# Attention matmuls cut from 256 to 128 columns, and the merge's loads given other tiles and another place

## The chip, the cores and the metric

The kernel runs on one core of a Trainium2 chip. The time is device microseconds of one execution of the whole program; several executions are made and the median is quoted. Beside them one execution is profiled, and all views of the profile are of that execution. TensorE is the matrix engine (PE in the profile, its weight loads PEld), VectorE is DVE, ScalarE is ACT, GpSimd is POOL, and SyncE (SP) issues most of the DMAs.

## The reference

One decoder layer on a sequence of 1024 rows of width 1024, in float32. Cut to what matters here:

```python
xn = rmsnorm(x, norm_mix_w)
da_q, da_k, da_v, sw_q, sw_k, sw_v, g_da, g_sw = split_cols(xn @ w_in)
y_da = diff_attention(da_q, da_k, da_v, lam, lam_init, subln_w)   # 4 heads, causal, two softmaxes each
y_sw = sliding_window_attention(sw_q, sw_k, sw_v, sinks)          # 8 heads, window 128
merged = sigmoid(g_da) * (y_da @ w_br_da) + sigmoid(g_sw) * (y_sw @ w_br_sw)
x = x + merged @ w_mix_out
x = x + conv_ffn(rmsnorm(x, norm_ffn_w), w_up, conv_w, conv_b, w_down)
out = rmsnorm(x, norm_final_w)
```

In the first attention a query block of 128 rows sees all keys up to its own block; in the second, its own block and the one before, and the first block only itself.

## The kernel before

Everything is held transposed, channels on the 128 partitions and the 1024 rows along the free axis. A float32 matrix product is made of rounded operands (type fp32r): each operand is split into a high part, which is the value rounded to fp32r by a ScalarE copy, and a low part, which is the value less the high part, a VectorE subtraction. A product is then three matmuls: high by high, high by low, low by high.

The stages follow each other: the projections; the two attentions, with some of the gates' projections (`back_half`, tiles `g`, lines L212 to L214) strewn between as filler for TensorE; the merge (`rest`); the mixing product; the hidden layer; the way down; the last norm. Within a stage a scheduler sets the order of each engine's instructions. It goes by the order in the code, by priorities (`high_priority`), and by when it reckons operands to be ready, so that an edit in one place can reorder rows far around it. Each engine, and each DMA queue, then runs its instructions strictly in that order.

The attention runs six units. Units 0 to 3 are the heads of the first attention. For each of the eight query blocks `da_step` makes scores for both softmaxes (tile `sc`, L639), masks and scales them on VectorE (L643), exponentiates on ScalarE (L644), joins the two (L649), transposes the result on TensorE (L655) and splits it into the tile `aT` (L657, L658). After each second block `da_av` multiplies the pair of blocks, 256 queries wide, by the values (L667 to L669). Of the pair, the earlier block sees one key block less. So in the last key block the first 128 of the 256 columns of `aT` hold nothing; `da_at` has GpSimd write zeros there (L622), and all 256 are multiplied. For the first query block, scores of 256 columns are made though 128 are read (`cuts`). Units 4 and 5 are the second attention: `sw_step` makes 256 columns of scores for each of four heads (L727), also in the first block, where 128 are read.

The merge reads the attention's results back from DRAM (`yd`) into raw tiles `yr` and splits them into `yh` (ScalarE, L836) and `yl` (VectorE, L837): chunks 0 to 3 are the first attention's, 4 to 7 the second's. There are four `yr` tiles, so chunk 4's load waits until chunk 0 is split. For each of eight output blocks m, `first(m)` loads the two gates (tiles `gr`, L796), multiplies them by the row norm on GpSimd (L797), takes the sigmoid (L804), makes the first branch's product (tile `sc`, for m = 0 with the products of the low parts last, L199 to L203) and multiplies it by its gate (L808). `second(m)` makes the second branch's product in two halves (tile `g`, two banks) and multiplies each by its gate (L816), adds the branches (L821) and splits the sum into `mh` and `ml` (L822, L823). `first(0)` and `first(1)` are written ahead of `second(0)`. Gate, result and weight loads all stand in SP's queue; `load_w` (L167, L177, L179) loads and splits a weight block.

Of the kernel before, what the change touches and what calls it, by code (L numbers as in the profile page):

```python
# [10 lines left out]
F32 = mybir.dt.float32  # L11
# [6 lines left out]
P = 128  # L18
D = 1024
T = 1024  # L20
KC = D // P
NB = T // P
H2 = 512
# [21 lines left out]
class Trunk:  # L45
# [568 lines left out]
    def da_at(self, r):  # L614

        t = {}
        for g in range((2 * r + 2 + 3) // 4):
            for part in range(2):
                t[g, part] = self.tl(self.ap, [P, 4, 256], "aT", F32R, bufs=5)
        for part in range(2):  # L620
            j = 2 * r + 1
            self.nc.gpsimd.memset(t[j // 4, part][:, j % 4, 0:P].bitcast(F32), 0.0)  # L622
        return t

    def da_step(self, h, i, st, aT):
        nc, ap = self.nc, self.ap
        q, k = st
        slope = 4.0 ** -(h + 1)
        w = (i + 1) * P

        lo = P if w == 640 else 0
        cuts = ((0, 256),) if i == 0 else ((0, w),) if w <= H2 else ((0, H2 - lo), (H2 - lo, w))
        pr = []
        for c in range(2):
            sc = self.tl(self.psS, [P, T], "sc")
            qs = q[c][:, i * P:(i + 1) * P]
            for part in range(2):
                for n0, n1 in cuts:
                    nc.tensor.matmul(sc[:, lo + n0:lo + n1], qs, k[c][part][:, n0:n1], start=part == 0, stop=part == 1)  # L639
            L = self.tl(ap, [P, T], "L", bufs=4)  # L640
            s = self.tl(self.st, [P, 4], "sm", bufs=8)
            o = 896 - i * P
            nc.vector.tensor_tensor_reduce(L[:, :w], sc[:, lo:lo + w], self.bias[:, o:o + w], slope, 3e38, ALU.add, ALU.min, s[:, 0:1])  # L643
            nc.scalar.activation(L[:, :w], L[:, :w], AF.Exp, bias=s[:, 0:1], scale=-1.0, accum_out=s[:, 1:2] if c else self.s0[:, i:i + 1])  # L644
            pr.append(L)

        nc.vector.reciprocal(s[:, 2:3], s[:, 1:2])
        nc.vector.tensor_scalar(s[:, 3:4], self.s0[:, i:i + 1], s[:, 2:3], self.neglam, ALU.mult, ALU.mult)
        nc.vector.scalar_tensor_tensor(pr[0][:, :w], pr[1][:, :w], s[:, 3:4], pr[0][:, :w], ALU.mult, ALU.add)  # L649
        qo = (i % 2) * P  # L650
        for j0 in range(0, i + 1, 4):
            nj = min(4, i + 1 - j0)
            ps = self.tl(self.psT, [P, 4, P], "t")
            for j in range(nj):
                nc.tensor.transpose(ps[:, j, :], pr[0][:, (j0 + j) * P:(j0 + j + 1) * P], self.ident)  # L655
            hi, lo = aT[j0 // 4, 0], aT[j0 // 4, 1]
            nc.scalar.copy(hi[:, :nj, qo:qo + P], ps[:, :nj, :])  # L657
            nc.vector.tensor_tensor(lo[:, :nj, qo:qo + P], ps[:, :nj, :], hi[:, :nj, qo:qo + P].bitcast(F32), ALU.subtract)  # L658

    def da_av(self, h, r, aT, y):  # L660
        nc = self.nc
        vh, vl = self.vhl
        ps = self.tl(self.psT, [P, H2], "t")
        nj = 2 * r + 2
        for j in range(nj):
            hi, lo = aT[j // 4, 0][:, j % 4, :], aT[j // 4, 1][:, j % 4, :]
            nc.tensor.matmul(ps[:, :256], vh[:, j, :], hi, start=j == 0, stop=False)  # L667
            nc.tensor.matmul(ps[:, :256], vh[:, j, :], lo, start=False, stop=False)  # L668
            nc.tensor.matmul(ps[:, :256], vl[:, j, :], hi, start=False, stop=j == nj - 1)  # L669
        nc.scalar.copy(y[:, r * 256:(r + 1) * 256], ps[:, :256])  # L670

    def da_norm(self, h, y):
# [43 lines left out]
    def sw_step(self, g, n, st):  # L716
        nc, ap = self.nc, self.ap
        q, k = st
        k0 = max(n - 1, 0) * P
        w = P if n == 0 else 256  # L720
        bo = T + (P if n == 0 else 0)
        sc = self.tl(self.psS, [P, 4, 256], "sc")
        s = self.tl(self.st, [P, 4, 4], "sw", bufs=4)
        L = self.tl(ap, [P, 4, 256], "L", bufs=4)
        for h in range(4):
            for part in range(2):
                nc.tensor.matmul(sc[:, h, :], q[h][:, n * P:(n + 1) * P], k[part][:, k0:k0 + 256], start=part == 0, stop=part == 1)  # L727
        for h in range(4):
            slope = 2.0 ** -(4 * g + h + 1)
            nc.vector.tensor_tensor_reduce(L[:, h, :w], sc[:, h, :w], self.bias[:, bo:bo + w], slope, 3e38, ALU.add, ALU.min, s[:, 0, h:h + 1])  # L730
        sink = self.vecs[:, C_SINK + 4 * g:C_SINK + 4 * g + 4]
        nc.vector.tensor_tensor(s[:, 0, :], s[:, 0, :], self.nsink[:, 4 * g:4 * g + 4], ALU.min)
        nc.vector.tensor_tensor(s[:, 1, :], s[:, 0, :], sink, ALU.add)
        nc.scalar.activation(s[:, 1, :], s[:, 1, :], AF.Exp)
        for h in range(4):
            nc.scalar.activation(L[:, h, :w], L[:, h, :w], AF.Exp, bias=s[:, 0, h:h + 1], scale=-1.0, accum_out=s[:, 2, h:h + 1])
        nc.vector.tensor_tensor(s[:, 2, :], s[:, 2, :], s[:, 1, :], ALU.add)
        self.last = nc.vector.reciprocal(s[:, 3, :], s[:, 2, :])
        for h in range(4):
            eng = nc.gpsimd if h in (3,) else nc.vector  # L740
            eng.tensor_scalar(L[:, h, :w], L[:, h, :w], s[:, 3, h:h + 1], None, ALU.mult)
        po = self.tl(self.psT, [P, H2], "t")
        nblk = w // P
        parts = []
        for b in range(nblk):
            ps = self.tl(self.psT, [P, 4, P], "t")
            for h in range(4):
                nc.tensor.transpose(ps[:, h, :], L[:, h, b * P:(b + 1) * P], self.ident)
            pt = self.tl(ap, [P, 2, 4, P], "aT", F32R, bufs=5)
            hi, lo = pt[:, 0], pt[:, 1]  # L750
            nc.scalar.copy(hi, ps)
            nc.vector.tensor_tensor(lo, ps, hi.bitcast(F32), ALU.subtract)
            parts.append((hi, lo))
        for b, (hi, lo) in enumerate(parts):
            kb = k0 // P + b
            va = self.vsw[kb // 4][:, kb % 4, g]
            for m, pt in enumerate((hi, lo)):
                nc.tensor.matmul(po, va, pt, start=b == 0 and m == 0, stop=b == nblk - 1 and m == 1)
        t = self.tl(self.gpool, [P, 4, P], "g", bufs=2)[0:64]
        nc.scalar.copy(t, po[64:128].rearrange("p (h q) -> p h q", h=4))  # L760
        pv = po[0:64].rearrange("p (c e q) -> p c e q", c=2, e=2)
        tv = t.rearrange("p (c e) q -> p c e q", e=2)
        y = self.tl(ap, [P, 2, P], "ys", bufs=3)
        for e in range(2):
            nc.vector.tensor_tensor(y[64 * e:64 * e + 64], pv[:, :, e], tv[:, :, e], ALU.add)
        self.store(self.yd[4 + 2 * g:6 + 2 * g, :, n * P:(n + 1) * P].rearrange("c p q -> p c q"), y)


    def rest(self, gctx):
        nc, tc = self.nc, self.tc  # L770
        with ExitStack() as ctx:
# [3 lines left out]
            with gctx, ExitStack() as bctx:  # L775
                yrp = bctx.enter_context(tc.tile_pool(name="yrp", bufs=4, reuse_waits="tile"))
                yp = bctx.enter_context(tc.tile_pool(name="yp", bufs=1, reuse_waits="tile"))
                bp = bctx.enter_context(tc.tile_pool(name="bp", bufs=2, reuse_waits="tile"))
                parts = []
                for c in range(8):  # L780
                    with tc.high_priority(200):
                        r = self.tl(yrp, [P, T], "yr")
                        nc.sync.dma_start(r, self.yd[c])
                    parts.append(self.split(*(yp.tile([P, T], F32R, name=f"y{p}{c}") for p in "hl"), r))
                    if self.back[7][0]:
                        self.back_half(*self.back[7][0].pop(0))
# [4 lines left out]
                def first(m):  # L791
                    w = self.next_w()
                    gs = []
                    for br in range(2):
                        g = self.tl(bp, [P, T], "gr", bufs=4)
                        nc.sync.dma_start(g, self.gd[8 * br + m])  # L796
                        i = nc.gpsimd.tensor_tensor(g, g, self.rstd, ALU.mult)  # L797
                        if m == 0:

                            tc.add_manual_dep(i.ins, self.last.ins.name, mybir.DependencyInfo(mybir.DependencyClass.Sync, mybir.DependencyReason.DATA),  # L800
                                              reason="softmax first")

                        with tc.issue_after(self.hi.ins) if br else nullcontext():
                            nc.scalar.activation(g, g, AF.Sigmoid)  # L804
                        gs.append(g)
# [654 lines left out]
```

## Time and profile before

| | us |
|---|---|
| median of three runs | 1337.81 (1337.39 to 1337.92) |
| the profiled execution's own time | 1339.47 |
| its span, from the first to the last instruction | 1337.7 |
| busy: TensorE, weight loads | 1319.4, 1096.8 |
| busy: VectorE, ScalarE, GpSimd | 1075.5, 624.4, 483.1 |
| granted TensorE clock, share of full | 0.997 |

The first attention's scores run from about 256 to 390 us, the second's from 390 to 481, and the merge's branch products from 506 to about 597. A row of the timeline gives the start, the time taken, engine, line, operation, the tile written and the tiles read, partitions by elements, the count where equal neighbours are merged, and in brackets how long the engine idled before and what released it. Matmuls overlap in the pipeline: one of 512 columns lasts 0.39 us, while the next one starts 0.23 us after it.

### The profile page before, as it was taken

How to read it: one execution, taken by the hardware profiler on the slowest of the kernel's cores; microseconds unless marked ns; L12 is line 12 of the kernel's file. 1: busy time of each engine (PE TensorE's matmuls, PEld its weight loads, DVE VectorE, ACT ScalarE, POOL GpSimd, SP SyncE). 2: the span in 40 equal slices, each digit the busy share in tenths (PEclk: the TensorE clock that was granted, in tenths of full speed). 3: DMA queues.
4: the chain of work that ended last, by engine and by line, in shares of the span. 5: the costliest groups of instructions: out<-in, count | busy, mean ns of one | idle time of the engine just before them, and what ended most of it. 6: DMA issues, size and time to landing. Idle time of an engine off the chain costs nothing.

```text
span 1337.7 us, 17292 instructions
## 1 busy us (share of the span) xinstructions
PE 1319.4 (99%) x6264; PEld 1096.8 (82%) x6264; DVE 1075.5 (80%) x1607; ACT 624.4 (47%) x1023; POOL 483.1 (36%) x363
## 2 busy tenths in 40 slices
PE   7999999999999999999999999999999999999997
PEld 6888888888888777888888888888888888888887
DVE  8847775289889877765678999999999997879975
ACT  8432232176667766433445443344444444323553
POOL 0336543000102113521436556555565520214532
PEclk9999999999999999999999999999999999999998
DMA  7423443866553335434432222222222229672263
GB/s 259 145 107 142 158 158 142 251 179 174 157 128 125 104 112 212 149 117 132 136 111 84 90 93 82 80 78 95 79 96 75 75 84 332 214 279 67 95 173 126
DMA packets 63621, 183.69 MB, mean 137 GB/s; under 512 B 6960, under 2 KB 15280, under 8 KB 63536
## 3 DMA queue, kind: packets, MB, share of 16 engines
q1 hardware_dynamic: 51504, 164.13, 37.5%
q10 hardware_dynamic: 11456, 17.41, 3.6%
q0 software_dynamic: 576, 1.05, 0.5%
q8 instruction: 49, 0.80, 0.3%
q14 instruction: 36, 0.29, 0.1%
HBM read 130.66 MB, written 50.86 MB: 136 GB/s over the span
## 4 chain that ended last, share of the span: by engine, by line
PE 93%; DVE 3%; POOL 1%; issue 1%; DMA 1%; ACT 1%; POOLq 0%; SPq 0%; ACTq 0%; DVEq 0%
PE t L924 13%; PE t L923 13%; PE t L925 13%; PE g L212 4%; PE g L213 4%; PE g L214 4%; PE sc L213 3%; PE sc L214 3%; PE sc L212 3%; PE t L917 3%; PE sc L639 3%; PE y L1167 2%; PE d L1167 2%; PE d L924 2%; PE d L923 2%; PE d L925 2%
## 5 line engine op out<-in xcount | busy, mean ns | idle before, releaser
L1097 ACT ACTIVATE c<-us,vecs 128x512 f32<-128x512 f32 x80 | 61.3, 781 | 134.0 <-POOL us L1091 130.0
L1099 DVE SCALAR_TENSOR_TENSOR c<-us,vecs,c 128x512 f32<-128x512 f32 x160 | 110.5, 748 | 8.6 <-ACT c L1097 8.6
L1091 POOL TENSOR_TENSOR us<-us,rstd 128x1024 f32<-128x1024 f32 x38 | 99.7, 2643 | 4.5 <-DVE us L472 2.4
L129 DVE TENSOR_TENSOR sl<-sf,sh 128x1024 fp32r<-128x1024 f32 x62 | 86.6, 1399 | 11.5 <-ACT sh L128 11.5
L128 ACT CAST sh<-sf 128x1024 fp32r<-128x1024 f32 x62 | 63.4, 1049 | 59.8 <-PE t L924 43.5
L129 DVE TENSOR_TENSOR wl<-raw,wh 128x1024 fp32r<-128x1024 f32 (+1 forms) x35 | 76.6, 2190 | 3.7 <-ACT wh L128 3.6
L177 ACT CAST wh<-raw 128x1024 fp32r<-128x1024 f32 (+2 forms) x46 | 46.2, 1005 | 67.8 <-PE sc L213 30.4
L104 POOL TENSOR_TENSOR sf<-rv 128x512 f32<-128x512 f32 x30 | 41.3, 1377 | 100.7 <-DVE sl L129 57.8
L212 PE MATMUL g<-xh,wh 128*128 128x512 f32 x176 | 70.7, 402 | 0.1
L214 PE MATMUL g<-xh,wl 128*128 128x512 f32 x176 | 70.4, 400 | 0.0
L213 PE MATMUL g<-xl,wh 128*128 128x512 f32 x176 | 70.2, 399 | 0.0
L179 DVE TENSOR_TENSOR wl<-raw,wh 128x1024 fp32r<-128x1024 f32 (+2 forms) x46 | 53.8, 1169 | 17.5 <-PE t L609 11.0
L109 POOL TENSOR_TENSOR sf<-raw,rv 128x512 f32<-128x512 f32 x30 | 40.8, 1359 | 66.0 <-DVE sl L129 66.0
L643 DVE CUSTOM_DVE_ANT_0 L<-sc,bias 128x128 f32<-128x128 f32 (+7 forms) x64 | 47.8, 752 | 17.0 <-PE sc L639 13.9
L622 POOL MEMSET aT<- 128x128 f32 x32 | 6.2, 205 | 151.6 <-PE t L668 97.9
L797 POOL TENSOR_TENSOR gr<-gr,rstd 128x1024 f32<-128x1024 f32 x16 | 41.0, 2566 | 52.9 <-DMA gr<-gd 43.5
L644 ACT ACTIVATE L<-L,sm 128x128 f32<-128x128 f32 (+7 forms) x64 | 49.6, 779 | 20.0 <-DVE sm L643 13.5
L129 DVE TENSOR_TENSOR wl<-rv,wh 128x512 fp32r<-128x512 f32 x30 | 49.8, 1661 | 3.5 <-ACT wh L128 3.5
L1101 ACT ACTIVATE c<-c 128x512 f32<-128x512 f32 x40 | 24.0, 600 | 60.7 <-DVE c L1099 60.7
L639 PE MATMUL sc<-u,u 128*128 128x512 f32 (+2 forms) x192 | 49.7, 358 | 0.0
L878 POOL TENSOR_TENSOR rstd<-rstd,t 128x512 f32<-128x512 f32 x14 | 21.7, 1558 | 76.1 <-ACT t L877 76.1
L212 PE MATMUL sc<-mh,wh 128*128 128x512 f32 x126 | 49.0, 389 | 0.0
(529 smaller groups left out, 4423.6 us busy)
## 6 DMA issues: line engine op xcount, KB each, us to landing
u<-qd SPq DMA_DIRECT2D x72, 256.0 KB, 6.2
raw<-in_w_in SPq DMA_DIRECT2D x25, 512.0 KB, 4.1
raw<-in_w_up SPq DMA_DIRECT2D x23, 512.0 KB, 3.5
hr<-hd SPq DMA_DIRECT2D x46, 256.0 KB, 5.7
hd<-c SPq DMA_DIRECT2D x22, 512.0 KB, 2.6
rv<-in_w_up SPq DMA_DIRECT2D x21, 512.0 KB, 3.5
raw<-in_w_down SPq DMA_DIRECT2D x19, 512.0 KB, 4.1
gr<-gd SPq DMA_DIRECT2D x16, 512.0 KB, 4.0
```

The source lines that it names most:

```text
L128: i = nc.scalar.copy(hi, src)
L129: j = nc.vector.tensor_tensor(lo, src, hi.bitcast(F32), ALU.subtract)
L212: nc.tensor.matmul(ps, wh[:, kc + o, :], ah, start=first and n == 0, stop=False)
L213: nc.tensor.matmul(ps, wh[:, kc + o, :], al, start=False, stop=False)
L214: nc.tensor.matmul(ps, wl[:, kc + o, :], ah, start=False, stop=last and n == len(kcs) - 1)
L639: nc.tensor.matmul(sc[:, lo + n0:lo + n1], qs, k[c][part][:, n0:n1], start=part == 0, stop=part == 1)
L923: nc.tensor.matmul(ps, ah[:, k, :], bh, start=first and n == 0, stop=False, skip_group_check=skip)
L924: nc.tensor.matmul(ps, ah[:, k, :], bl, start=False, stop=False, skip_group_check=skip)
L925: i = nc.tensor.matmul(ps, al[:, k, :], bh, start=False, stop=last and n == len(ks) - 1, skip_group_check=skip)
L1091: (nc.vector if j == 0 else nc.gpsimd).tensor_tensor(u[:, 2:], u[:, 2:], self.rstd, ALU.mult)
L1097: nc.scalar.activation(c, u[:, o + 2:o + 2 + H2], AF.Identity, bias=self.vecs[:, C_CB + m:C_CB + m + 1], scale=col(m, 2))
L1099: nc.vector.scalar_tensor_tensor(c, u[:, o + k:o + k + H2], col(m, k), c, ALU.mult, ALU.add)
```

## The change

Three things are edited.

First, the last key block's value products in `da_av` read and write only the 128 columns that are used, the zeros in `da_at` go, and the scores of the first query block are made 128 wide in both attentions.

Second, the raw tiles of chunks 4 to 7 come from a pool of their own (`ysp`, four tiles), so that they don't wait for the splits of chunks 0 to 3.

Third, the gates of m = 0 and m = 1 are loaded together, at a higher priority, ahead of chunk 4's load; `first` uses these tiles.

```diff
@@ da_at
-        for part in range(2):
-            j = 2 * r + 1
-            self.nc.gpsimd.memset(t[j // 4, part][:, j % 4, 0:P].bitcast(F32), 0.0)
@@ da_step
-        cuts = ((0, 256),) if i == 0 else ((0, w),) if w <= H2 else ((0, H2 - lo), (H2 - lo, w))
+        cuts = ((0, w),) if w <= H2 else ((0, H2 - lo), (H2 - lo, w))
@@ da_av
-            hi, lo = aT[j // 4, 0][:, j % 4, :], aT[j // 4, 1][:, j % 4, :]
-            nc.tensor.matmul(ps[:, :256], vh[:, j, :], hi, start=j == 0, stop=False)
-            nc.tensor.matmul(ps[:, :256], vh[:, j, :], lo, start=False, stop=False)
-            nc.tensor.matmul(ps[:, :256], vl[:, j, :], hi, start=False, stop=j == nj - 1)
+            c = slice(P if j == nj - 1 else 0, 256)
+            hi, lo = aT[j // 4, 0][:, j % 4, c], aT[j // 4, 1][:, j % 4, c]
+            nc.tensor.matmul(ps[:, c], vh[:, j, :], hi, start=j == 0, stop=False)
+            nc.tensor.matmul(ps[:, c], vh[:, j, :], lo, start=False, stop=False)
+            nc.tensor.matmul(ps[:, c], vl[:, j, :], hi, start=False, stop=j == nj - 1)
@@ sw_step
-                nc.tensor.matmul(sc[:, h, :], q[h][:, n * P:(n + 1) * P], k[part][:, k0:k0 + 256], start=part == 0, stop=part == 1)
+                nc.tensor.matmul(sc[:, h, :w], q[h][:, n * P:(n + 1) * P], k[part][:, k0:k0 + w], start=part == 0, stop=part == 1)
@@ rest
+                ysp = bctx.enter_context(tc.tile_pool(name="ysp", bufs=4, reuse_waits="tile"))
                 parts = []
+                gates = {}
                 for c in range(8):
+                    if c == 4:
+                        with tc.high_priority(300):
+                            for m in range(2):
+                                gates[m] = [self.tl(bp, [P, T], "gr", bufs=4) for _ in range(2)]
+                                for br, g in enumerate(gates[m]):
+                                    nc.sync.dma_start(g, self.gd[8 * br + m])
                     with tc.high_priority(200):
-                        r = self.tl(yrp, [P, T], "yr")
+                        r = self.tl(ysp if c > 3 else yrp, [P, T], "yr")
                         nc.sync.dma_start(r, self.yd[c])
@@ rest, first
-                        g = self.tl(bp, [P, T], "gr", bufs=4)
-                        nc.sync.dma_start(g, self.gd[8 * br + m])
+                        if m in gates:
+                            g = gates[m][br]
+                        else:
+                            g = self.tl(bp, [P, T], "gr", bufs=4)
+                            nc.sync.dma_start(g, self.gd[8 * br + m])
```

The order of the engines' instructions changes as follows. On TensorE, at the first pair of blocks of head 0, this stood before (`t` is the product, `aT` the transposed weights of the softmax, `v` the values, high and low):

```order
L668 MATMUL t_2014<-aT_1968,v_1949 128x256
L669 MATMUL t_2014<-aT_1967,v_1950 128x256
L667 MATMUL t_2014<-aT_1967,v_1949 128x256
L668 MATMUL t_2014<-aT_1968,v_1949 128x256
L669 MATMUL t_2014<-aT_1967,v_1950 128x256
```

The same place now, with line numbers two lower:

```order
L666 MATMUL t_2012<-aT_1968,v_1949 128x256
L667 MATMUL t_2012<-aT_1967,v_1950 128x256
L665 MATMUL t_2012<-aT_1967,v_1949 128x128
L666 MATMUL t_2012<-aT_1968,v_1949 128x128
L667 MATMUL t_2012<-aT_1967,v_1950 128x128
```

The number of matmuls is the same; the last key block's three are half as wide. Counted over the program, 48 value products and 32 scores are 128 wide now, and all 80 were 256 wide before. The order of the rows around them differs on TensorE, VectorE and ScalarE all through the attention.

On SP's queue, at the merge, gates and results stood like this before (the first two `gr` are the gates of m = 0, the next two those of m = 1; the `yr` are chunks 4 to 7):

```order
L796 DMA gr_5078<-gd 128x1024
L796 DMA gr_5082<-gd 128x1024
L783 DMA yr_5044<-yd 128x1024
L783 DMA yr_5050<-yd 128x1024
L783 DMA yr_5056<-yd 128x1024
L783 DMA yr_5062<-yd 128x1024
L796 DMA gr_5118<-gd 128x1024
L796 DMA gr_5122<-gd 128x1024
```

And now:

```order
L786 DMA gr_5015<-gd 128x1024
L786 DMA gr_5016<-gd 128x1024
L786 DMA gr_5019<-gd 128x1024
L786 DMA gr_5020<-gd 128x1024
L789 DMA yr_5023<-yd 128x1024
L789 DMA yr_5029<-yd 128x1024
L789 DMA yr_5035<-yd 128x1024
L789 DMA yr_5041<-yd 128x1024
```

The second pair of gates moved ahead of the four result loads. On VectorE, from chunk 3's split on, before:

```order
L837 TENSOR_TENSOR yl_5041<-yr_5038,yh_5040 128x1024
L179 TENSOR_TENSOR wl_5076<-raw_5072,wh_5074 128x1024
L837 TENSOR_TENSOR yl_5047<-yr_5044,yh_5046 128x1024
L837 TENSOR_TENSOR yl_5053<-yr_5050,yh_5052 128x1024
L837 TENSOR_TENSOR yl_5059<-yr_5056,yh_5058 128x1024
L837 TENSOR_TENSOR yl_5065<-yr_5062,yh_5064 128x1024
L808 TENSOR_TENSOR gr_5078<-gr_5078,sc_5086 128x1024
L808 TENSOR_TENSOR gr_5118<-gr_5118,sc_5126 128x1024
L816 TENSOR_TENSOR gr_5082<-gr_5082,g_5152 128x512
```

And now:

```order
L846 TENSOR_TENSOR yl_5012<-yr_5009,yh_5011 128x1024
L179 TENSOR_TENSOR wl_5055<-raw_5051,wh_5053 128x1024
L817 TENSOR_TENSOR gr_5015<-gr_5015,sc_5061 128x1024
L846 TENSOR_TENSOR yl_5026<-yr_5023,yh_5025 128x1024
L846 TENSOR_TENSOR yl_5032<-yr_5029,yh_5031 128x1024
L846 TENSOR_TENSOR yl_5038<-yr_5035,yh_5037 128x1024
L817 TENSOR_TENSOR gr_5019<-gr_5019,sc_5097 128x1024
L846 TENSOR_TENSOR yl_5044<-yr_5041,yh_5043 128x1024
L825 TENSOR_TENSOR gr_5016<-gr_5016,g_5123 128x512
```

The two products of the first branch with their gates (L808 before, L817 now) stand between the splits of chunks 4 to 7 instead of behind them.

## The prediction

> **What bounds the kernel now.** I read the page first (span, busy times, the chain), then the stretches around the two places of the change, then who TensorE waits for.
>
> ```profile
> span 1337.7 us, 17292 instructions
> ...
> PE 1319.4 (99%) x6264; PEld 1096.8 (82%) x6264; DVE 1075.5 (80%) x1607; ACT 624.4 (47%) x1023; POOL 483.1 (36%) x363
> ...
> PE 93%; DVE 3%; POOL 1%; issue 1%; DMA 1%; ACT 1%; POOLq 0%; SPq 0%; ACTq 0%; DVEq 0%
> ```
>
> TensorE is busy for 99% of the span and carries 93% of the chain that ended last. The stretches show that this holds in the attention (240 to 500 us), the merge's head (500 to 530) and the rest of the merge:
>
> ```profile
> core 0: us, PE busy (x) PEld busy (x) DVE busy (x) ACT busy (x) POOL busy (x), PEclk, DMA share, GB/s
> 240.00:390.00 150.00, 149.92 (x902) 129.65 (x901) 111.80 (x288) 91.11 (x212) 10.64 (x32) 1.00 0.64 175
> 390.00:500.00 110.00, 108.30 (x616) 88.39 (x615) 94.50 (x333) 76.54 (x219) 17.62 (x19) 1.00 0.41 121
> 500.00:530.00 30.00, 28.12 (x123) 22.63 (x122) 20.51 (x17) 17.64 (x18) 10.43 (x4) 1.00 0.60 224
> 530.00:600.00 70.00, 70.00 (x311) 57.95 (x310) 50.51 (x42) 27.62 (x27) 30.55 (x12) 1.00 0.39 135
> ```
>
> In the attention TensorE idles 0.08 + 1.70 = 1.8 us of 260; in the merge's head 1.9 of 30. So what a matmul costs there is paid in full, and all the waits the change can take away are those few us. The clock is 1.00 throughout. The merge's loss is one wait, in the list of who waited for whom and in TensorE's timeline:
>
> ```profile
> PE g L212 <- DVE gr L816: 1.7, 1, 1.7
> ```
>
> ```profile
> 522.91 0.39 PE L214 MATMUL g<-yh,wl 128*128 128x512 f32 x1
> 525.03 0.50 PE L212 MATMUL g<-yh,wh 128*128 128x512 f32 x1 [1.73 <-DVE gr L816]
> ```
>
> **The narrow matmuls.** The order counts 48 value products (4 heads, 4 block pairs, 3 products) and 32 scores (16 of each attention) that go from 256 to 128 columns: 80, with no matmul removed and each weight load kept. What a matmul costs is the distance from its start to the next start. Merged rows of equal matmuls give it: total less one duration, over the count less one. The means by shape, the one line of the column sums, and four such rows of the timeline:
>
> ```profile
> L213 PE MATMUL sc<-ml,wh 128*128 128x512 f32 x126 | 49.0, 389 | 0.0
> L669 PE MATMUL t<-aT,v 128*128 128x256 f32 x80 | 22.6, 282 | 0.0
> L655 PE MATMUL t<-ident,L 128*128 128x128 f32 x144 | 22.2, 274 | 0.1
> ```
>
> ```profile
> L220 PE MATMUL t<-ones,sq x64: 165/250/250, 298.7 to 406.9; 128*128 128x1 f32 x64
> ```
>
> ```profile
> 249.73 1.03 PE L609 MATMUL t<-ident,f 128*128 128x128 f32 x8
> ...
> 300.58 0.95 PE L220 MATMUL t<-ones,sq 128*128 128x1 f32 x8
> ...
> 393.63 0.88 PE L727 MATMUL sc<-u,u 128*128 128x256 f32 x6
> ...
> 510.01 1.98 PE L203 MATMUL sc<-yl,wh 128*128 128x512 f32 x8
> ```
>
> 512 columns: (1.98 - 0.39)/7 = 0.227 us. 256 columns: (0.88 - 0.28)/5 = 0.120. A transpose of 128 columns: (1.03 - 0.27)/7 = 0.109. A sum of one column: (0.95 - 0.25)/7 = 0.100. So below 256 columns the distance hardly falls, even with 1 column: each of these has its own weight load ahead. This caps the gain: at the transposes' 0.109 the change saves 80 x (0.120 - 0.109) = 0.9 us. If the loads did not bound it, 128 columns would take half of the step from 256 to 512 (0.107/2) plus the fixed 0.013 that is left of 0.120: 0.067, and the gain would be 4.2 us.
>
> The other end is a loss. The trace has no rounded (fp32r) matmul under 256 columns. Its two narrow kinds, both plain 32-bit, last longer than a line through the wide ones: from 389 and 282 ns the line falls 0.418 ns a column to a foot of 175; one column should last 175 and lasts 250, 128 columns should last 229 and the transposes last 274. So something is charged in narrow 32-bit matmuls that the wide rounded ones don't pay. If a narrow rounded operand is streamed in several passes as an unrounded one would be, four passes of 128 columns are 512 columns: the 512-wide row's 0.227, and the change costs 80 x (0.227 - 0.120) = 8.6 us. I take this end: the sums are the nearest row in kind (no transpose, narrow), and 75 ns over the line at one column fits several short passes better than one. It remains a judgement; both ends stay in the range. The Trainium skill (FP8 and Floating Point Precision, TensorE Precision Notes) gives four passes to true FP32 alone and lets the reduced form read and truncate its operand; by it the narrow matmuls cost no more, and the term is at or below zero. No row here shows which holds under 256 columns. The Trainium skill (TensorE: Matmul & The Clock Gate, Back-to-back issue gap) gives about 81 ns for 128 columns with loads; an estimate by that page is a gain of 3.1 us.
>
> Of the 8.6 us the idle 1.8 us in the attention can swallow some; I take half, 0.9. Net +7.7.
>
> **The memsets.** 32 on POOL go:
>
> ```profile
> L622 POOL MEMSET aT<- 128x128 f32 x32 | 6.2, 205 | 151.6 <-PE t L668 97.9
> ```
>
> POOL waits for TensorE there, and nothing on TensorE's list waits for a memset: zero. If the 6.2 us did hold VectorE somewhere, at most TensorE's idle 1.8 us could come back.
>
> **The merge's loads.** The second gate pair's loads move ahead of the last four result loads, and those have four raw tiles of their own, so they no longer wait for the first four splits. Before:
>
> ```profile
> 494.98 3.57 SPq L796 DMA_DIRECT2D gr<-gd  x2
> 506.58 3.73 SPq L783 DMA_DIRECT2D yr<-yd  x4
> 510.41 1.17 SPq L796 DMA_DIRECT2D gr<-gd  x2
> ```
>
> ```profile
> 500.69 4.79 POOL L797 TENSOR_TENSOR gr<-gr,rstd 128x1024 f32<-128x1024 f32 x2 [7.44 <-DMA gr<-gd]
> 518.74 5.64 POOL L797 TENSOR_TENSOR gr<-gr,rstd 128x1024 f32<-128x1024 f32 x2 [13.26 <-DMA gr<-gd]
> ...
> 534.12 6.49 POOL L797 TENSOR_TENSOR gr<-gr,rstd 128x1024 f32<-128x1024 f32 x2 [1.36 <-DMA gr<-gd]
> ```
>
> ```profile
> 523.16 1.22 DVE L808 TENSOR_TENSOR gr<-gr,sc 128x1024 f32<-128x1024 f32 x1 [2.25 <-ACT gr L804]
> 524.30 1.28 DVE L816 TENSOR_TENSOR gr<-gr,g 128x512 f32<-128x512 f32 x2
> ```
>
> What is removed: the second pair lands late (POOL waits for it till 518.74), its sigmoid is late, VectorE's second L808 waits for that, and L816, queued behind it, frees TensorE's bank late. The gap is 525.03 - 522.91 = 2.12, of which 0.23 is the matmul: 1.9 us gained. With early gates only L808's own product is waited for.
>
> What it adds: the second pair now lands right behind the first. Loads of this kind land 4.0 us after issue:
>
> ```profile
> gr<-gd SPq DMA_DIRECT2D x16, 512.0 KB, 4.0
> ```
>
> Issued by about 499, they land by 503, and POOL multiplies four tiles in a row from 500.7, just where VectorE makes the low halves of the first attention's results (yl), which TensorE takes from 510.0 on (L203). These two disturb each other:
>
> ```profile
> 503.23 6.74 DVE L837 TENSOR_TENSOR yl<-yr,yh 128x1024 fp32r<-128x1024 f32 x4 [3.56 <-ACT yh L836]
> ```
>
> ```profile
> 503.23 3.33 DVE L837 TENSOR_TENSOR yl<-yr,yh 128x1024 fp32r<-128x1024 f32 x1 [3.56 <-ACT yh L836]
> ```
>
> ```profile
> 533.76 1.21 DVE L179 TENSOR_TENSOR wl<-raw,wh 128x1024 fp32r<-128x1024 f32 x1
> 534.96 3.37 DVE L823 TENSOR_TENSOR ml<-gr,mh 128x1024 fp32r<-128x1024 f32 x1
> ```
>
> The first yl takes 3.33 us where a subtraction of this size takes 1.21: it ends 1.1 after POOL's second multiply (500.69 + 4.79 = 505.48). At 534 to 541 they alternate: ml (3.37) sits out a multiply, and POOL's pair takes 6.49 for 4.79. So I let them take turns, 1.1 and 2.3 us: yl 1 ends at 506.6, multiply 3 at 508.9, yl 2 at 510.0, multiply 4 at 512.3, yl 3 at 513.4, yl 4 at 514.5, against 503.23 + 6.74 = 509.97 before. TensorE's eight L203 end by 511.8 before; the last two need yl 4, so they end at 514.5 + 0.45 = about 514.9: 3.0 us lost. The weight split behind yl 4 (wl, 1.2) ends at 515.7, the next product's third matmul asks for it at 515.4: 0.2 more. Merge: 3.0 + 0.2 - 1.9 = +1.3 us, between -1.9 (no collision) and +3.2 (the old wait stays). The Trainium skill (SBUF — State Buffer, Who interferes with whom) speaks against this edit: it has a two-input VectorE instruction and a reading GpSimd one hold a shared port pair exclusively. By it the term is the +1.3; with no lock it would be -1.9; the 3.33 and the 3.37 agree with it.
>
> **Sum.** 8.6 - 0.9 + 1.3 = +9.0 us on a span of 1337.7. The profiled run took 1339.47, 1.8 beside its span and 1.7 over the median of 1337.81 of the runs shown; the difference carries over: 1337.8 + 9.0 = 1346.8 us.
>
> **The rivals.** *Narrow is dear, no collision*: if the second gates land after yl 4 (past 510), POOL is out of the way; 8.6 - 0.9 - 1.9 = +5.8, 1343.6 us. For: DMA is busy at 0.60 there. Against: 4.0 us to land. *Narrow is free, collision stays*: -0.9 + 1.3 = +0.4, 1338.2 us. For: nothing shows a rounded matmul in passes. *Faster*: narrow matmuls at 0.109 and no collision, -0.9 - 1.9 = -2.8, 1335.0 us; at 0.067 even with the collision -4.2 + 1.3 = -2.9, or with neither 1331.7. It decides where a narrow matmul starts its follower in under 0.120 - 1.3/80 = 0.104 us with the collision, 0.144 without. Against: the transposes' 0.109 and the sums' 0.100 look like a floor. *The new order stalls*: the attention's VectorE and ScalarE rows are in another order throughout; two waits as long as the longest of TensorE there now (1.7) would add 3.4 to the forecast: 1350.2 us.
>
> **How the numbers follow.** 0.2% of 1337.8 is 2.7 us, about what a measurement of this kernel tells from no change. Chances: forecast 0.50, dear without collision 0.20, stalls 0.08 (all slower, 0.78); free with collision 0.09 (same); faster 0.13. The range reaches from 1337, just under the free case, to 1351, over the stalled one; it leaves out the faster case and a little above.
>
> **What would show it.** In the profile after, a row of merged 128-wide score or value matmuls: a distance of 0.227 confirms the first term, 0.11 refutes it and with it most of the forecast. In the merge, yl rows of 3 us and L203 reaching past 514 (shifted by what the attention costs) confirm the collision; yl at 1.2 refutes it. The 1.7 us wait for L816 should be gone in either case. If TensorE's idle time in the attention grows by over 2 us, the order, not the width, cost the time.

## The result, and the profile after

The changed kernel takes 1346.45 us (median of 6 runs, 1345.69 to 1347.61), the kernel before 1337.6 on the same chip (1336.44 to 1338.07). The ratio is 1.0064 (95% interval 1.0054 to 1.0075): 8.6 us slower, between 7.2 and 10.0. That is the predicted total, but not made of the predicted parts. Further down, differences in us are ratios times 1337.8; parts of a span come from one profiled execution each. That of after took 1345.98 us, that of before 1339.47, so the spans differ by 6.5 us only.

The page's span and its chain, after:

```profile
span 1344.2 us, 17215 instructions
...
PE 90%; DVE 4%; DMA 2%; ACT 2%; issue 1%; POOL 1%; POOLq 0%; SPq 0%; ACTq 0%; DVEq 0%
```

TensorE's share of the chain falls from 93% to 90%; DMA and ScalarE have 2% each where they had 1%. So new waits have come onto the path. The first starts of three kinds of matmul in TensorE's timeline say where:

| first start (us) | before | after | more |
|---|---|---|---|
| scores of the attention, `sc<-u,u` | 256.8 | 256.8 | 0 |
| first product of the merge, `sc<-yh,wh` | 506.4 | 512.5 | 6.1 |
| mix, `sc<-mh,wh` | 595.9 | 603.6 | 7.7 |
| end of the span | 1337.7 | 1344.2 | 6.5 |

The attention lost 6.1 us and the merge 1.6; 1.2 us came back over the 740 us of the rest, which the change doesn't touch.

**The width is not the cause.** TensorE's timeline has merged rows of 128-wide scores of the second attention:

```profile
392.70 0.98 PE L725 MATMUL sc<-u,u 128*128 128x128 f32 x7
441.85 0.87 PE L725 MATMUL sc<-u,u 128*128 128x128 f32 x6
```

The groups by shape give the duration of one, 280 ns:

```profile
L725 PE MATMUL sc<-u,u 128*128 128x128 f32 x16 | 2.7, 280 | 0.0
```

So the distance is (0.98 - 0.28)/6 = 0.117 us and (0.87 - 0.28)/5 = 0.118. Over the 65 places where one of the narrow matmuls, value products among them, is followed by another matmul of 128 columns, the median is 0.111. The wide ones had 0.120. The forecast's first term needed 0.227.

The median hides two prices. TensorE's timeline at the first pair of blocks, where two wide value products go ahead of the three narrow ones:

```profile
273.44 0.28 PE L666 MATMUL t<-aT,v 128*128 128x256 f32 x1
273.56 0.28 PE L667 MATMUL t<-aT,v 128*128 128x256 f32 x1
273.67 0.22 PE L665 MATMUL t<-aT,v 128*128 128x128 f32 x1
273.73 0.28 PE L666 MATMUL t<-aT,v 128*128 128x128 f32 x1
273.84 0.27 PE L667 MATMUL t<-aT,v 128*128 128x128 f32 x1
```

The first narrow one starts its follower after 0.06 us, the second after 0.11. It is so at all 16 such places: 0.06, then 0.11 to 0.12.

**What the attention waits for.** The same two stretches of the attention as in the prediction, after the change, and the list of who TensorE waited for from 238 to 612 us (the sum of the waits, how many, the longest):

```profile
240.00:390.00 150.00, 148.04 (x890) 126.63 (x889) 113.92 (x293) 90.80 (x213) 5.54 (x6) 1.00 0.64 174
390.00:500.00 110.00, 107.03 (x605) 87.08 (x604) 91.72 (x325) 74.40 (x214) 17.69 (x18) 0.99 0.37 110
```

```profile
PE sc L203 <- DVE yl L846: 2.1, 1, 2.1
PE sc L636 <- DMA u<-qd: 0.9, 2, 0.5
PE t L746 <- ACT aT L749: 0.7, 1, 0.7
PE t L746 <- DVE L L739: 0.7, 1, 0.7
PE t L652 <- DVE aT L655: 0.6, 1, 0.6
PE t L652 <- DVE L L646: 0.5, 2, 0.3
...
```

Before, the list from 238 us to the start of the merge had two entries:

```profile
PE t L758 <- DVE aT L752: 0.5, 2, 0.3
PE t L748 <- DVE L L741: 0.3, 1, 0.3
```

TensorE's idle time in the two stretches grew from 0.08 + 1.70 to 1.96 + 2.97 us: 3.2 us more. The waits in the attention are short, at most 0.7 us, and most of them stand ahead of the transposes of the softmax rows (L652, L746). The idle time counts whole gaps only. Adding up every distance between neighbouring matmuls that exceeds the usual one for its width (0.228 us for 512 columns, 0.173 for 384, 0.119 for 256, 0.109 for 128, and 0.028 from the last transpose of a group to another kind), what is lost ahead of these transposes goes from 5.2 us to 11.5.

**The merge.** The rows that answer to those of before, on VectorE, GpSimd, TensorE and SP's queue:

```profile
509.38 11.02 DVE L846 TENSOR_TENSOR yl<-yr,yh 128x1024 fp32r<-128x1024 f32 x4 [3.81 <-ACT yh L845]
```

```profile
506.72 11.46 POOL L806 TENSOR_TENSOR gr<-gr,rstd 128x1024 f32<-128x1024 f32 x4 [8.82 <-DMA gr<-gd]
```

```profile
519.32 2.35 PE L203 MATMUL sc<-yl,wh 128*128 128x512 f32 x4 [2.09 <-DVE yl L846]
```

```profile
502.93 1.96 SPq L786 DMA_DIRECT2D gr<-gd  x4
```

The four gates now go out together, GpSimd multiplies four tiles in a row (11.46 us), and VectorE's four splits beside it take 11.02 us instead of 6.74. TensorE waits 2.09 us for the last ones, and the wait for L816 (1.7 before) is off the list.

**A halved clock.** The granted clock of after is 0.50 in two stretches; each row with the stretch of the same length ahead of it:

```profile
495.29:498.70 3.41, 2.32 (x8) 1.03 (x8) 2.97 (x7) 3.26 (x9) 0.99 (x1) 1.00 0.00 0
498.70:502.10 3.40, 3.40 (x11) 2.71 (x12) 1.92 (x4) 0.47 (x1) 0.00 (x0) 0.50 0.67 176
515.78:519.19 3.41, 1.45 (x7) 0.87 (x5) 3.41 (x2) 3.41 (x5) 2.40 (x1) 1.00 0.85 265
519.20:522.60 3.40, 3.28 (x7) 2.26 (x8) 3.22 (x4) 2.35 (x3) 0.00 (x0) 0.50 0.43 169
```

TensorE was busy for 2.32 and 1.45 of the 3.41 us ahead, and then ran 3.4 us at half speed: at worst 1.7 us of work lost each time. The kernel before shows no such stretch in the attention or the merge. What this did to the time of after isn't shown: of its six runs the two with the lowest mean clock (0.995) took 1345.7 and 1346.0 us, the three with 0.997 took 1346.6 to 1347.6.

### The profile page after: what moved, and what is told of

The parts are those of the page before. It is cut to its first block, busy times and chain, and to the rows that moved or that the text cites. A ratio compares the mean times of both kernels' runs of the same rounds, so it can differ in the third digit from the quotient of the medians.

```text
span 1344.2 us, 17215 instructions
## 1 busy us (share of the span) xinstructions
PE 1322.6 (98%) x6264; PEld 1097.2 (82%) x6264; DVE 1082.9 (81%) x1607; ACT 623.3 (46%) x1023; POOL 480.3 (36%) x331
## 4 chain that ended last, share of the span: by engine, by line
PE 90%; DVE 4%; DMA 2%; ACT 2%; issue 1%; POOL 1%; POOLq 0%; SPq 0%; ACTq 0%; DVEq 0%
PE t L934 13%; PE t L932 13%; PE t L933 13%; PE g L212 3%; PE g L213 3%; PE g L214 3%; PE sc L213 3%; PE sc L214 3%; PE sc L212 3%; PE t L926 3%; PE y L1176 2%; PE d L1176 2%; PE sc L636 2%; PE d L932 2%; PE d L933 2%; PE d L934 2%
## 5 line engine op out<-in xcount | busy, mean ns | idle before, releaser
L129 DVE TENSOR_TENSOR sl<-sf,sh 128x1024 fp32r<-128x1024 f32 x62 | 87.5, 1413 | 11.5 <-ACT sh L128 11.5
L232 POOL TENSOR_TENSOR rs<-ms,mhalf 128x8 f32<-128x8 f32 (+2 forms) x9 | 14.6, 1621 | 218.7 <-DVE sm L644 144.2
L739 POOL TENSOR_SCALAR L<-L,sw 128x256 f32<-128x256 f32 (+1 forms) x16 | 14.9, 932 | 104.9 <-DVE sw L736 75.5
L636 PE MATMUL sc<-u,u 128*128 128x512 f32 (+3 forms) x192 | 48.7, 355 | 0.9 <-DMA u<-qd 0.9
```

The source lines that it names most:

```text
L129: j = nc.vector.tensor_tensor(lo, src, hi.bitcast(F32), ALU.subtract)
```

## The experiments

Two theories. **A, the order:** the attention's instructions are put in order by a scheduler that sees the narrow tiles; the new order leaves less work between a softmax row's steps and its transposes, and TensorE waits. **B, the width:** narrow matmuls are dear. Beside both stands the collision of GpSimd and VectorE in the merge. The expectations call the runs by short names, which stand below in brackets; each ratio is to the kernel before on the same chip.

### Narrow matmuls in the old order

(`held_narrow`) After the scheduling, each of the 80 matmuls is replaced in its place by one of half the width, with the same waits and signals:

```diff
+def _halve(nc, half):
+    for x, cols in half:
+        o, (mov, sta) = x.outs[0].bass_ap, (y.bass_ap for y in x.ins)
+        m = nc.tensor.matmul(o[:, cols], sta, mov[:, cols], start=x.start_tensor_calc, stop=x.stop_tensor_calc)
+        ...
+        b.instructions[n] = m.ins
```

> The kernel before with every instruction in its old place on every engine and with its old waits; only the 80 matmuls of the attention are cut from 256 to 128 columns, after the order has been set. Nothing else is changed (the memsets stay, the merge is as before). Theory A (the order: narrower tiles gave the attention another order, and that order waits more): the narrow matmuls start 0.111 us apart where the wide ones start 0.120 apart, 80 x 0.009 = 0.7 us less, so -0.7 us, between -1.0 and 0 against the kernel before. Theory B (the width: narrow matmuls are dear, the first term of the prediction): +8.6 us as forecast, or at least the +6.2 us that the attention lost.

Measured: 1337.3 us, ratio 0.9997 (0.9989 to 1.0006): -0.4 us (-1.5 to +0.8). Theory B's +6.2 to +8.6 is out. In this kernel's timeline all narrow matmuls carry line 1439, where they are put in:

```profile
392.54 0.83 PE L1439 MATMUL sc<-u,u 128*128 128x128 f32 x6
```

(0.83 - 0.28)/5 = 0.110 us apart. But 0.7 us was too little for the narrowing: added up over the 80 places, the distances to the followers are 8.6 us here and 10.6 in the kernel before, 2.1 less, because some of the followers start after 0.06 us. Its profiled attention (first score to first merge product) takes 248.6 us against 249.6 before, so about half of that arrives; the rest goes into other distances. It loses 5.4 us ahead of the transposes, close to the 5.2 before.

### The attention's edits alone

(`attn_only`) `da_at`, `da_step`, `da_av` and `sw_step` as in the change, `rest` as before.

> Only the attention's part of the change: narrow scores and value products, no memsets; the merge as before. Its instructions stand in the changed kernel's order, but for some 30 rows. Theory A and theory B alike: the attention's +6.2 us return, the merge stays, so +6.2 us (5 to 7.5) against the kernel before. If it comes near 0, the loss in the attention needs the merge's earlier loads, and both theories are wrong.

Measured: 1344.35 us, ratio 1.0054 (1.0041 to 1.0066): +7.2 us (5.5 to 8.8). So most of the loss needs nothing of the merge's edits. The profile shows less of it than the medians: the attention takes 253.8 us (+4.2) and the merge 90.3 (+0.8), and the profiled execution of the kernel before was itself 1.7 us over its median. TensorE waits in the attention for much the same things as after the change (238 to 513 us):

```profile
PE t L746 <- ACT aT L749: 0.7, 1, 0.7
PE t L746 <- DVE L L739: 0.7, 1, 0.7
PE t L652 <- DVE aT L655: 0.6, 1, 0.6
PE sc L636 <- DMA u<-qd: 0.5, 1, 0.5
...
```

### Wide matmuls in the new order

(`wide_new_order`) The reverse of the first: scheduled narrow, widened in place. `wide` makes 256 columns of an operand again, beginning the given number of columns earlier; the value products then read another block, so the result isn't the attention's.

```diff
+    for x, back in half:
+        o, (mov, sta) = x.outs[0].bass_ap, (y.bass_ap for y in x.ins)
+        o, mov = wide(o, back), wide(mov, 3 * back)
+        ...
```

> The reverse of held_narrow: the attention is put in order with the narrow matmuls, as in attn_only (PE's and VectorE's rows are attn_only's), and only then the 80 matmuls are given 256 columns again; the merge as before, and the memsets stay. In the 48 value products among the 80 the moving operand is the block before, whose columns are all written, so the attention's result is another one; their number, width and place are what counts here. Theory A (the order): attn_only's +7.2 us and 80 x 0.009 = 0.7 us for the width: +7.9 us (6 to 9) against the kernel before. Theory B (the width): all matmuls have the widths of before, so within 1 us of it.

Measured: 1343.69 us, ratio 1.0045 (1.0032 to 1.0059): +6.0 us (4.3 to 7.9). The widths are those of before and the loss is there: the order alone makes it. Its profile agrees: the attention takes 253.9 us where the same widths in the old order took 249.6, and 10.4 us are lost ahead of the transposes instead of 5.2. That the time lies 1.9 us under the sum written down, and 1.2 under the narrow kernel of the same order, is within the two intervals. It keeps the memsets; so they don't carry the loss either.

### Part of the narrowing

(`sw_only`, `av_only`) Only `sw_step`'s scores (16 matmuls), and only `da_av`'s value products without the memsets (48).

> Only the sliding-window scores are narrow, 16 of the 80 matmuls; some 200 rows of PE's order change. Theory B (width): in proportion to the matmuls, 16/80 of attn_only's +7.2 us, +1.4 us. Theory A (order): no proportion; the time follows what TensorE loses ahead of the transposes of the softmax rows (5.2 us over the usual distances before, 11.2 us in attn_only): if this loss is near 5 us, within 1 us of before, and if it is near 11 us, +6.

> Only the value products are narrow, 48 of the 80 matmuls, and the memsets are gone; some 480 rows of PE's order change. Theory B (width): 48/80 of +7.2 us, +4.3 us. Theory A (order): no proportion; the time follows the loss ahead of the transposes as in sw_only.

Measured: 1342.25 us, ratio 1.0033 (1.0020 to 1.0046), +4.4 us (2.7 to 6.2) for 16 matmuls; 1339.88 us, ratio 1.0017 (1.0008 to 1.0026), +2.3 us (1.1 to 3.5) for 48. The +1.4 and the +4.3 of theory B lie outside. No proportion, as A has it. The finer part of the expectation holds only roughly:

| | before | held | only `sw_step` | only `da_av` | wide, new order | attention's edits | after |
|---|---|---|---|---|---|---|---|
| profiled attention (us) | 249.6 | 248.6 | 251.7 | 252.6 | 253.9 | 253.8 | 255.8 |
| lost ahead of the transposes (us) | 5.2 | 5.4 | 8.2 | 9.3 | 10.4 | 11.2 | 11.5 |

The attention's time follows this loss through the first six columns to within about 1 us; the medians of the two partial kernels stand in the other sequence (+4.4 and +2.3). For `sw_step` alone the profiled attention is only 2.0 us longer than before; that execution, 1340.70 us, was the shortest of the five, so about half of the median's loss isn't seen in it. After has 2.0 us more than the attention's edits alone. It has the half-clock stretch at 498.7, which that kernel lacks, but no run shows that this is the reason.

### The merge's edits alone

(`merge_only`) `rest` as in the change, the attention as before.

> Only the merge's part of the change: raw tiles of their own for the second attention's results, and the first two rows' gates loaded ahead of them. The attention has the old order. With the collision (GpSimd's gate multiplies beside VectorE's splits, the third term of the prediction): +1.3 us as forecast, +1.6 by the changed kernel's own trace, 0.8 to 2.0. Without it, the removed wait of 1.9 us is all there is: -1.9 us.

Measured: 1340.83 us, ratio 1.0019 (1.0010 to 1.0028): +2.5 us (1.3 to 3.7), above the forecast's 1.3. The profiled merge takes 91.4 us against 89.5. The collision is there without any change in the attention:

```profile
503.76 10.68 DVE L848 TENSOR_TENSOR yl<-yr,yh 128x1024 fp32r<-128x1024 f32 x4 [3.58 <-ACT yh L847]
```

```profile
PE sc L203 <- DVE yl L848: 2.2, 2, 1.8
```

```profile
511.57:514.98 3.41, 1.26 (x5) 0.74 (x5) 3.41 (x3) 3.41 (x5) 0.65 (x1) 1.00 0.92 372
514.98:518.39 3.41, 3.41 (x10) 2.62 (x9) 3.41 (x4) 1.48 (x2) 0.00 (x0) 0.51 0.50 131
```

The wait of 2.2 us is followed by 3.4 us at half clock. 2.2, and up to 1.7 for the clock, less the removed 1.9, makes up to +2.0, where the forecast had 3.0 + 0.2 - 1.9. The runs themselves fall apart by their mean granted clock: the three with 0.998 took 1338.8 to 1339.2 us, the eight with 0.996 or 0.997 took 1340.3 to 1341.8. 3.41 us at half clock lower the mean by 0.0013, so the first three, some 1.3 us over the kernel before, look like the collision without the half-clock stretch. No run was made to separate the two.

### The second gates held until the splits are done

(`merge_late`) GpSimd's multiplies for m = 1 are made to wait for the low half of chunk 3:

```diff
+                    if c == 3:
+                        held = self.lo
...
+                        if m == 1:
+                            tc.add_manual_dep(i.ins, held.ins.name, ...)
```

> Merge's part of the change as in merge_only, and the second row's two gate multiplies on GpSimd wait for VectorE's split of the fourth chunk; the order on each engine is that of merge_only. Collision theory: the four splits take 6.7 to 8 us as before the change instead of 11.0, the first product of the merge does not wait for the last split, and the gain of the removed wait comes through: -1.9 us against the kernel before (-2.5 to -1.0), 3 us less than merge_only. If the 3 us between the fast and the slow merge have another cause (the loads' own traffic, their order in the queue), it is as slow as merge_only: +1.3 to +1.6.

Measured: 1337.7 us, ratio 1.0001 (0.9992 to 1.0010), 3.1 us less than the merge's edits alone: the collision was the cause of its loss. VectorE's four splits:

```profile
502.55 6.39 DVE L853 TENSOR_TENSOR yl<-yr,yh 128x1024 fp32r<-128x1024 f32 x4 [3.58 <-ACT yh L852]
```

But the expected gain of 1.9 didn't come. A new wait stands there, for the splits of chunks 4 to 7:

```profile
PE g L213 <- DVE yl L853: 0.8, 1, 0.8
```

That takes 0.8 of the 1.9 us that the removed wait could give; the 1.1 that are left are at the edge of the interval (-1.1 to +1.3), and the profiled merge is 1.2 us shorter than before (88.3 us against 89.5).

### A version that is faster than both

(`held_reorder`) The narrow matmuls held in the old order, and, with the loads of before, VectorE's late product moved behind the two that it held up (`last` is the second of them):

```diff
-                    nc.vector.tensor_tensor(gs[0], gs[0], ps, ALU.mult)
+                    if m == 1:
+                        after.append((gs[0], ps))
+                    else:
+                        nc.vector.tensor_tensor(gs[0], gs[0], ps, ALU.mult)
...
+                    if m == 0:
+                        g0, ps0 = after.pop()
+                        with tc.issue_after(last.ins):
+                            nc.vector.tensor_tensor(g0, g0, ps0, ALU.mult)
```

> held_narrow, and in the merge, with the loads of before, VectorE's product of the second row with its gate (L808 in the kernel before) is queued behind the first row's two second products (L816), no longer ahead of them; PE's order is held_narrow's. The late gate should then hold up nobody: TensorE's wait for L816 (1.9 us in the kernel before, 1.2 us in held_narrow) is gone, without GpSimd's multiplies beside the splits. Sum: -0.4 measured for held_narrow and -1.2 to -1.9: -2.0 us against the kernel before (-2.5 to -1.2). If another wait takes its place (as a wait of 0.8 us did in merge_late): -0.4 to -1.0.

Measured: 1335.51 us, ratio 0.9982 (0.9973 to 0.9991): -2.4 us (-3.6 to -1.2). In the merge's head TensorE is never idle, and the clock stays full:

```profile
500.00:530.00 30.00, 30.00 (x134) 24.82 (x133) 21.82 (x20) 18.61 (x19) 9.64 (x4) 1.00 0.63 227
```

The second pair of gates still comes late (GpSimd multiplies it from 516.51); the two products of the first row (L828) no longer stand in the queue behind its product (L832). The new place of the product wasn't tried with the wide matmuls; against `held_narrow` it gives about 2 us.

```profile
516.51 5.67 POOL L806 TENSOR_TENSOR gr<-gr,rstd 128x1024 f32<-128x1024 f32 x2 [12.55 <-DMA gr<-gd]
...
519.15 0.69 DVE L828 TENSOR_TENSOR gr<-gr,g 128x512 f32<-128x512 f32 x1 [0.48 <-issue]
521.82 0.69 DVE L828 TENSOR_TENSOR gr<-gr,g 128x512 f32<-128x512 f32 x1 [1.98 <-PE g L215]
522.42 1.22 DVE L832 TENSOR_TENSOR gr<-gr,sc 128x1024 f32<-128x1024 f32 x1
```

## Why the prediction was right in its total and wrong in its largest term

**TensorE sets the time, and what it loses is paid in full:** right. The whole loss stands on TensorE.

**The narrow matmuls, +8.6:** wrong; -0.4 measured with the old order held (-1.5 to +0.8), which holds the other end of the term, -0.9. The step that failed is the choice between the ends: "I take this end". It took the 75 ns by which a one-column sum lasts longer than the line for four passes. But that is a duration, which overlaps the next matmul; the distances in the same rows (0.109 for 128 columns, 0.100 for one) showed no passes. The Trainium skill (FP8 and Floating Point Precision, TensorE Precision Notes) lets the reduced form off the four passes; the median of 0.111 us agrees, and the forecast should have followed it. The other estimate by the Trainium skill, from 81 ns (TensorE: Matmul & The Clock Gate, Back-to-back issue gap), was too hopeful: over the 80 places the mean distance was 0.107 in `held_narrow`, with a weight load ahead of each matmul. The floor that the prediction saw at the transposes' 0.109 doesn't hold either: followers after 0.06 us make the distances 2.1 us shorter together, where 0.9 was the cap.

**The idle time swallows 0.9:** fell with its term. The idle time didn't shrink, it grew by 3.2 us, past the 2 us named as the sign that "the order, not the width, cost the time".

**The order:** this was a rival with a chance of 0.08, "The new order stalls", priced at two waits of 1.7 us on top of the forecast. It was the cause of the attention's loss, by itself and without dear matmuls, and mis-sized: the attention's edits cost 7.2 us (5.5 to 8.8), as many waits of 0.7 us and less and not as two long ones. The prediction saw that the rows are in another order "throughout" and looked only for a long wait. Why the new order waits more is settled only in part. From 278 to 358 us the kernel before places 111 of the 512-wide fill matmuls (`g<-x`), the one after 91, `wide_new_order` 90; less cover between a softmax row and its transposes fits the waits. But with `sw_step` alone there are 111 there too, and its loss comes later. No run moved fill matmuls by themselves.

**The memsets, 0:** nothing speaks against it; with them in place the new order still cost 6.0 us. They weren't taken out by themselves.

**The merge, +1.3:** the mechanism is right. The splits slowed from 6.74 to 11.02 us, L203 reaches 521.67 (514.9 was forecast, and the attention is 6.1 late: 521.0), and the wait for L816 is gone. The size was low: 1.6 in the profile after, +2.5 (1.3 to 3.7) alone. The halved clock behind the wait was missing from the sum. There is a slip in it too: its own times, 514.9 against 511.8 and 515.7 against 515.4, make 3.1 and 0.3, so +1.5 and not +1.3; that changes nothing else.

**The sum:** 7.7 + 1.3 was forecast and about 7 + 2 came, with the 7 from another cause. The total fits by chance; a forecast from the prediction's other end, -0.9 and +1.3, would have said no change, and missed.

## What to carry to other kernels

Where a scheduler sets the order, an edit that makes instructions cheaper is also a new order for everything around them, and on an engine that is 99% busy the order can cost far more than the edit saves: price it by holding the old order and cutting only the widths. Read a matmul's price from the distance to its follower, never from its duration, and look at single distances too: a median of 0.111 us hid 19 of 65 at 0.06. An earlier load is a gain only if what it sets off has free engines to run on; often it is enough to take the work that isn't late out of the queue behind the one that is.

## What the runs showed of the hardware

After a stretch in which TensorE is idle for part of 3.41 us, the granted clock can be half for the next 3.41 us. It was seen behind 1.1 and 2.0 us of idle in 3.41 us (after), 2.2 (the merge's edits alone), and 0.8 us in the attention with only `da_av` narrow:

```profile
491.56:494.97 3.41, 2.65 (x9) 1.11 (x9) 2.81 (x7) 3.16 (x8) 0.98 (x1) 1.00 0.11 33
494.97:498.38 3.41, 3.41 (x11) 2.65 (x11) 1.98 (x4) 0.53 (x1) 0.00 (x0) 0.51 0.61 180
```

It wasn't seen behind the 1.9 us at 523 in the kernel before. Where the idle time lies may be a reason: if a trace has several half-clock stretches, they start a whole number of 3.41 us apart (the two of after 20.5 us, six times that). Counted back so from the half clock at the end of the kernel before (1329.75 us), its wait falls into two stretches, with 0.9 and 0.8 us of idle:

```profile
520.79:524.20 3.41, 2.51 (x12) 1.72 (x10) 1.16 (x2) 2.09 (x2) 3.41 (x2) 1.00 0.11 46
524.20:527.61 3.41, 2.58 (x11) 2.16 (x12) 3.38 (x5) 1.80 (x2) 0.18 (x1) 1.00 0.00 0
```

The idle time in one such stretch doesn't decide alone either: `held_narrow` has 1.2 us of it from 520.57 to 523.98 and full clock behind. What the four have in common is few columns: the matmuls that start in the stretch ahead of the half clock have 2048 to 2560 columns together, those in that one of `held_narrow` 4096. But `attn_only` has a stretch with 2432 (from 493.60) and full clock behind it, so this is a lead and not a rule. The Trainium skill (TensorE: Matmul & The Clock Gate, Part 1) describes a free-running activity window of about 3.4 us, after which the clock is halved or released; the lengths agree. The Trainium skill's advice to avoid idle gaps of over about 3 us (same page, Why this matters for your kernels) is too mild for these rows, where 2.1 us was the longest single wait ahead of a halved stretch.

A rounded 128-wide matmul with a weight load of its own, behind another narrow one, starts its follower after about 0.11 us, where a 256-wide one does so after 0.120. The first narrow value product behind a wide one does so after 0.06 us, so halving the columns saves half the distance once in a row of narrow matmuls and little after that: 2.1 of 10.6 us over the 80 places. The weight loads start 0.11 to 0.12 us apart in either case (from 273.44 to 273.78 us in after), and so look like what paces them; no run changes them by themselves.
